# One decoder layer on one core: layer norms worked in pairs of tiles, a start in half chunks behind constant products, and later state evacuations

## The chip, the cores and the metric

The kernel runs on one core of a Trainium2 chip. The metric is the device time of one execution in microseconds (us), as the median of several runs. The engines are TensorE (PE, with its weight loads as PEld), VectorE (DVE), ScalarE (ACT), GpSimd (POOL) and SyncE (SP), whose queue (SPq) issues DMA transfers.

## The reference, cut to what matters

One macaron layer with three post-norms, for 320 tokens (256 of a prompt and 8 x 8 samples) of width 2048:

```python
x <- LN1(alpha*x + 0.5*SwiGLU_1(x))
x <- LN2(alpha*x + W_out [ retention_heads(x) ; nsa_heads(x) ])
x <- LN3(alpha*x + 0.5*SwiGLU_2(x))
```

LN takes mean and variance over the 2048 features of each token, and applies a gain and an offset per feature. The outputs are y, the retention states of prompt and samples (`rsp`, `rss`), and the new cache rows. The layers between (compressed, selected and window attention, and the retention heads) are the same in both kernels.

## The kernel before

**Data.** Activations are held transposed: 16 tiles of 128 features x 320 tokens. Every float32 operand is cut into a high half (rounded by ScalarE, L219) and a low half (source minus high, VectorE, L220), and a product is three matmuls: high weight by high x, high weight by low x, low weight by high x (`mm3`, L213 to L215). Weights come in chunks of 128x1024 (512 KB) through SyncE's queue into a ring of four (`w_load`, L269), are split two chunks ahead (`w_split`), and feed 24 matmuls each: two feature tiles of x by four output tiles, one output tile after the other. Tiles `xh` and `xl` are the halves of x.

**Stages.** `all` runs in order: `start`, FFN1 (up sweeps, then four down sweeps), LN1, the compressed cache, the combined input projection and its heads, `w_out`, LN2, FFN2, LN3 and the store of y. A main generator writes the weight matmuls. Background tasks (`spawn`) are written between them when a planner's clock, a sum of assumed matmul times, has passed their due time (`tick`). `until` and `drain` run the tasks until a condition holds or none is left. So the written order is fixed when the program is built, and each engine follows its own list.

**A layer norm.** `ln_residual` makes d = coef*x for each of the 16 tiles. `ln_evac` (L456) adds the sweep's result from PSUM. `ln_accumulate` squares the tile (ScalarE, L436) and GpSimd adds tile and square into two accumulators (L444, L445); the last four tiles go to TensorE themselves. The sums over features are matmuls against a constant tile `ones` (1/256), in full float32 (L208): a pair (d and its square) for the accumulators and one for each of the last four tiles, ten in all, four of them written in the last sweep and six after it:

```python
            if j != 1:
                self.ln_sum()
...
        while self.ln_n < 5:
            self.ln_sum()
```

`ln_stats` then makes the centre `dl` (ScalarE, L513), its square (L515), the variance (VectorE, L517), the root (ScalarE, L519), subtracts `dl` from the first tiles (L522: the first on VectorE, the others on GpSimd) and takes the reciprocal `rs` (VectorE, L524). A tile is centred (`ln_center`, L528), scaled by gain and `rs` in one VectorE operation (`ln_scale`, L531), and for LN2 split with the offset added (`ln_split`, ScalarE L539 and VectorE L540).

LN1 is done by a background task with no tile ahead, and its tiles are scaled by `x_scale`. LN2 runs by `ln_tiles`: four steps ahead of FFN2, then three in front of each chunk (`pre`), centring on GpSimd. LN3 has 13 tiles ahead (12 on GpSimd), then per tile a scale, an offset (ScalarE L1843, every sixth on VectorE, L1841) and a 160 KB transfer (L1844).

**States.** `states` makes the samples' new retention states, four heads of eight batches: per two batches two products (TensorE) into one PSUM bank, and a VectorE evacuation of 128x512 that adds the decayed state (L1711). The last head waits for `ln2_begun`, and `drain` puts it wholly ahead of FFN2.

**Start.** x comes in eight transfers of two tiles, the first four weight chunks between them. The first two x tiles are split, then the whole first chunk (ScalarE 128x1024, then VectorE), then two more tiles and the second chunk. `ones` is written at the end of the first sweep (`constants`).

## Time and profile before

| | |
|---|---|
| median of 3 runs | 2848.97 us (2848.24 to 2850.14) |
| the profiled execution | 2848.41 us |
| its span on the core | 2846.8 us |
| mean granted clock of TensorE | 0.992 |
| TensorE busy | 2784.3 us, 98% |
| VectorE busy | 1555.9 us, 55% |
| ScalarE busy | 1205.5 us, 42% |
| GpSimd busy | 351.4 us, 12% |

The span runs from the first to the last event of the core in the profiled execution, and the device time holds a little more than it. Positions below are microseconds from the span's start. Start: 0 to 12. LN1's sums: 940 to 955. LN2: 1862 to 1895. LN3 and the store: 2817 to 2847.

### The profile page before, as it was taken

How to read it: one execution, taken by the hardware profiler on the slowest of the kernel's cores; microseconds unless marked ns; L12 is line 12 of the kernel's file. 1: busy time of each engine (PE TensorE's matmuls, PEld its weight loads, DVE VectorE, ACT ScalarE, POOL GpSimd, SP SyncE). 2: the span in 40 equal slices, each digit the busy share in tenths (PEclk: the TensorE clock that was granted, in tenths of full speed). 3: DMA queues.
4: the chain of work that ended last, by engine and by line, in shares of the span. 5: the costliest groups of instructions: out<-in, count | busy, mean ns of one | idle time of the engine just before them, and what ended most of it. 6: DMA issues, size and time to landing. Idle time of an engine off the chain costs nothing. (4 is left out here: it accounts for less than half of the span.)

```text
span 2846.8 us, 49623 instructions
## 1 busy us (share of the span) xinstructions
PE 2784.3 (98%) x19841; PEld 2708.5 (95%) x19841; DVE 1555.9 (55%) x1937; ACT 1205.5 (42%) x1668; POOL 351.4 (12%) x420
## 2 busy tenths in 40 slices
PE   9999999999999999999999999999999999999996
PEld 9999999999999989998888888989999999999996
DVE  4333333347867769783565555673333333367665
ACT  4333333345445546554344454343333333354553
POOL 0000000000112223223132111440000000001111
PEclk9999999999999999999999999999999999999998
DMA  6555444446556445537577764544444444444442
GB/s 226 179 193 180 152 149 148 150 161 194 201 172 227 142 139 156 147 126 267 189 245 235 239 219 142 205 144 148 151 151 151 149 149 151 152 145 147 151 151 89
DMA packets 202600, 484.74 MB, mean 170 GB/s; under 512 B 24257, under 2 KB 100930, under 8 KB 200450
## 3 DMA queue, kind: packets, MB, share of 16 engines
q1 hardware_dynamic: 192546, 451.30, 49.3%
q0 software_dynamic: 9824, 30.29, 3.1%
q8 instruction: 155, 2.54, 0.4%
q14 instruction: 75, 0.61, 0.1%
HBM read 467.47 MB, written 22.28 MB: 172 GB/s over the span
## 5 line engine op out<-in xcount | busy, mean ns | idle before, releaser
L220 DVE TENSOR_TENSOR wl<-raw,wh 128x1024 fp32r<-128x1024 f32 x650 | 815.5, 1255 | 1073.2 <-ACT wh L219 1052.4
L219 ACT ACTIVATE wh<-raw 128x1024 fp32r<-128x1024 f32 x650 | 688.0, 1059 | 1165.2 <-PE m L214 1125.1
L213 PE MATMUL m<-x,wh 128*128 128x320 f32 x3664 | 1148.6, 313 | 10.1 <-ACT wh L219 6.3
L214 PE MATMUL m<-x,wh 128*128 128x320 f32 x3664 | 1132.9, 309 | 4.3 <-DVE x L540 4.3
L215 PE MATMUL m<-x,wl 128*128 128x320 f32 x3664 | 1132.5, 309 | 0.4 <-DVE wl L220 0.4
L213 PEld LDWEIGHTS m<-x,wh 128*128 128x128 f32 x3664 | 690.6, 188 | 33.3 <-issue 22.0
L214 PEld LDWEIGHTS m<-x,wh 128*128 128x128 f32 x3664 | 690.8, 189 | 6.3 <-DVE x L540 5.6
L215 PEld LDWEIGHTS m<-x,wl 128*128 128x128 f32 x3664 | 690.3, 188 | 0.8 <-DVE wl L220 0.8
L213 PE MATMUL m<-r,wh 128*128 128x320 f32 (+1 forms) x1592 | 495.5, 311 | 2.3 <-ACT wh L219 1.0
L214 PE MATMUL m<-r,wh 128*128 128x320 f32 (+1 forms) x1592 | 487.8, 306 | 4.4 <-DVE r L220 4.4
L215 PE MATMUL m<-r,wl 128*128 128x320 f32 (+1 forms) x1592 | 490.8, 308 | 0.0
L213 PEld LDWEIGHTS m<-r,wh 128*128 128x128 f32 x1592 | 298.7, 188 | 8.4 <-issue 3.7
L214 PEld LDWEIGHTS m<-r,wh 128*128 128x128 f32 x1592 | 299.3, 188 | 6.7 <-DVE r L220 5.8
L215 PEld LDWEIGHTS m<-r,wl 128*128 128x128 f32 x1592 | 298.3, 187 | 0.0
L476 POOL TENSOR_TENSOR t<-x,x 128x320 f32<-128x320 f32 x3 | 2.7, 913 | 1415.0 <-DVE x L456 719.1
L220 DVE TENSOR_TENSOR r<-G,r 128x640 fp32r<-128x640 f32 (+1 forms) x184 | 158.0, 863 | 0.0
L213 PE MATMUL x<-r,G 128*128 128x256 f32 x480 | 137.8, 287 | 0.0
L214 PE MATMUL x<-r,G 128*128 128x256 f32 x480 | 135.7, 283 | 0.0
L215 PE MATMUL x<-r,G 128*128 128x256 f32 x480 | 135.3, 282 | 0.0
L219 ACT ACTIVATE r<-G 128x640 fp32r<-128x640 f32 (+1 forms) x184 | 130.1, 712 | 0.0
L220 DVE TENSOR_TENSOR r<-x,r 128x512 fp32r<-128x512 f32 (+1 forms) x76 | 79.2, 1049 | 36.5 <-ACT r L219 35.7
L213 PEld LDWEIGHTS x<-r,G 128*128 128x128 f32 x480 | 91.7, 191 | 1.1 <-issue 1.0
(384 smaller groups left out, 2246.7 us busy)
## 6 DMA issues: line engine op xcount, KB each, us to landing
raw<-wup SPq DMA_DIRECT2D x352, 512.0 KB
raw<-wdn SPq DMA_DIRECT2D x176, 512.0 KB
raw<-win_ret SPq DMA_DIRECT2D x48, 512.0 KB
raw<-win_nsa SPq DMA_DIRECT2D x40, 512.0 KB
raw<-wout SPq DMA_DIRECT2D x32, 512.0 KB
r<-pks SPq DMA_DIRECT2D x96, 128.0 KB
x<-pkc SPq DMA_DIRECT2D x152, 64.0 KB
K<-cw1k SPq DMA_DIRECT2D x16, 512.0 KB
```

What stands on the lines that cost most here:

```text
L213: mm(out, wh, xh, start=start, stop=False)
L214: mm(out, wh, xl, start=False, stop=False)
L215: mm(out, wl, xh, start=False, stop=stop)
L219: self.nc.scalar.activation(hi, src, AF.Copy)
L220: self.nc.vector.tensor_tensor(lo, src, hi.bitcast(F32), op=ALU.subtract)
L476: nc.gpsimd.tensor_tensor(s, self.d[0], self.d[1], op=ALU.add)
```

## The change

1. *Start.* The first chunk comes in two transfers of 512 columns, and is split in halves in alternation with the first two x tiles. `ones` is written first, and TensorE does eleven float32 products of it with itself (`WARM`) into a PSUM bank that is overwritten later.
2. *Sums.* VectorE adds tiles 12 to 14 into one, and squares 12 to 14 into one (four additions). TensorE does two sums in the last sweep and four after it: both for the mean first, then both for the squares.
3. *Pairs.* d is allocated by pairs of tiles. `ln_stats` centres three or four pairs ahead (the first on VectorE, the others on GpSimd), each by one 128x640 operation whose second operand is repeated (`twice`). Pairs are then centred and scaled by VectorE, and gain and offset are applied by ScalarE (`ln_affine`). For LN2 `ln_pairs` does the first pair tile by tile as before. For the later ones ScalarE makes the 640-wide high half and VectorE the low one by a subtraction. Three steps stand ahead of FFN2, then one in front of each chunk. For LN3 each pair leaves in one 320 KB transfer. LN1's tiles are still scaled one by one.
4. *States.* The last head's products are written as before, but its four evacuations stand 35 planner microseconds later and 3 apart; FFN2 begins when the products are written.

```diff
@@ start
         for q in range(8):
-            self.nc.sync.dma_start(out=self.xraw[q], in_=self.I["xT"][:, 2 * q:2 * q + 2, :])
-            if q < 4:
+            if q:
+                self.nc.sync.dma_start(out=self.xraw[q], in_=self.I["xT"][:, 2 * q:2 * q + 2, :])
+            else:
+                r, w = self.raw[:, 0], self.wq[0]
+                self.nc.sync.dma_start(out=self.xraw[0], in_=self.I["xT"][:, 0:2, :])
+                for k in range(2):
+                    self.nc.sync.dma_start(out=r[:, 512 * k:512 * k + 512], in_=w[:, 512 * k:512 * k + 512])
+                self.raws[0], self.n_dma = r, 1
+            if 0 < q < 4:
                 self.w_load()
-        for q in range(2):
-            self.x_split(q)
-            self.w_split()
+        self.ones = self.t([128, 128], "ones")
+        self.nc.vector.memset(self.ones, 1.0 / 256.0)
+        ps = self.p("m3")
+        for _ in range(WARM):
+            self.nc.tensor.matmul(ps[:, 0:128], self.ones, self.ones, start=True, stop=True)
+        hi, lo = (self.t([128, 1024], t, F32R) for t in ("wh0", "wl0"))
+        r = self.raws.pop(0)
+        for k in range(2):
+            c = slice(512 * k, 512 * k + 512)
+            self.split(self.xh[k], self.xl[k], self.xraw[0][:, k])
+            self.split(hi[:, c], lo[:, c], r[:, c])
...
+        self.x_split(1)
+        self.w_split()
@@ ln_residual
+        for p in range(KT // 2):
...
+            d = self.x_room(self.kl, [128, 2, NT])
+            self.pairs[p] = d
@@ ln_accumulate
-        if m >= 12:
+        if m == 12:
+            self.ln_last = [(self.d[m], sq)]
+        elif m == 13:
+            t = self.t([128, NT], "t", bufs=NTMP)
+            nc.vector.tensor_tensor(t, self.ln_last[0][0], self.d[m], op=ALU.add)
+            nc.vector.tensor_tensor(sq, self.ln_last[0][1], sq, op=ALU.add)
+            self.ln_last = [(t, sq)]
+        elif m == 14:
+            t, q = self.ln_last[0]
+            nc.vector.tensor_tensor(t, t, self.d[m], op=ALU.add)
+            self.ln_q = q, sq
+        elif m == 15:
+            q, r = self.ln_q
+            nc.vector.tensor_tensor(q, q, r, op=ALU.add)
             self.ln_last.append((self.d[m], sq))
@@ ln_evac
-            if j != 1:
-                self.ln_sum()
+                for ps, src in zip(self.ln_sums, (self.acc_d, self.acc_q)):
+                    self.mm(ps[:, :NT], self.ones, src, True, False, 0.54)
@@ ln_stats
-    def ln_stats(self, eps, ahead=4):
+    def ln_stats(self, eps, ahead=3):
-        while self.ln_n < 5:
-            self.ln_sum()
+        for k, last in ((0, False), (0, True), (1, False), (1, True)):
+            self.mm((p1, p2)[k][:, :NT], self.ones, self.ln_last[last][k], False, last, 0.54)
-        for m in range(ahead):
-            d = self.d[m]
-            (nc.gpsimd if m else nc.vector).tensor_tensor(d, d, self.dl, op=ALU.subtract)
+        for p in range(ahead):
+            self.ln_center_pair(p, nc.gpsimd if p else nc.vector)
+    def twice(self, a):
+        return a.rearrange("p (o t) -> p o t", o=1).to_broadcast([128, 2, NT])
+    def ln_center_pair(self, p, engine):
+        d = self.pairs[p]
+        engine.tensor_tensor(d, d, self.twice(self.dl), op=ALU.subtract)
+    def ln_scale_pair(self, p):
+        if p >= self.ln_ahead:
+            self.ln_center_pair(p, self.nc.vector)
+        d = self.pairs[p]
+        self.nc.vector.tensor_tensor(d, d, self.twice(self.rs), op=ALU.mult)
+    def ln_affine(self, m, col, out, engine=None):
+        scale, bias = (self.vecs[:, c + m:c + m + 1] for c in (col, col + KT))
+        if engine is None:
+            self.nc.scalar.activation(out, self.d[m], AF.Identity, bias=bias, scale=scale)
+        else:
+            engine.tensor_scalar(out, self.d[m], scale, bias, op0=ALU.mult, op1=ALU.add)
@@ ln_tiles becomes ln_pairs
+    def ln_pairs(self, col):
...
+        for p in range(n + 1):
+            if p < n:
+                h = highs[p] = self.x_room(self.kh, [128, 2, NT], F32R)
...
+                    if p:
+                        self.ln_affine(m, col, y[p][:, k])
+                    else:
+                        self.ln_scale(m, col, y[p][:, k])
+                        nc.scalar.activation(h[:, k], y[p][:, k], AF.Identity, bias=self.ln_offset(m, col))
+                if p:
+                    nc.scalar.activation(h, y[p], AF.Copy)
...
+            q = p - 1
+            if q >= 0:
...
+                if q:
+                    nc.vector.tensor_tensor(l, y.pop(q), h.bitcast(F32), op=ALU.subtract)
...
+            if p + 1 < n:
+                self.ln_scale_pair(p + 1)
+            yield
@@ states
+                banks.append((b, pb))
+                if h < 3:
+                    self.state_out(h, sin, banks)
+                    yield 1.5
+            if h == 3:
+                self.states_begun = True
+                yield 35.0
+                while banks:
+                    self.state_out(h, sin, banks)
+                    yield 3.0
@@ all
-        tiles = self.ln_tiles(32)
-        for _ in range(4):
-            next(tiles)
+        pairs = self.ln_pairs(32)
+        for _ in range(3):
+            next(pairs)
         self.ln2_begun = True
-        self.drain()
+        self.until(lambda: self.states_begun)
         def pre(c):
-            for _ in range(3):
-                next(tiles, None)
+            next(pairs, None)
...
-        self.ln_stats(1, 13)
...
+        self.ln_stats(1, 4)
+        for p in range(KT // 2):
+            self.ln_scale_pair(p)
+            for m in (2 * p, 2 * p + 1):
+                self.ln_affine(m, 64, self.d[m], nc.vector if m == KT - 1 else None)
+            nc.sync.dma_start(out=self.O["y"][:, 2 * p:2 * p + 2], in_=self.pairs[p])
```

TensorE at the end of LN2's last sweep. Names of matmuls are `result<-moving,constant`; m is the last output tile, `t` and `x` are the squares and tiles of d, G are the states' operands. Before:

```order
L215 MATMUL m_1649_19639<-x_952_13377,wl_1651_19647 128x320
L208 MATMUL x_1657_19718<-x_1478_18290,ones_367 128x320
L208 MATMUL x_1658_19719<-t_19729,ones_367 128x320
L208 MATMUL x_1657_19718<-x_1481_18331,ones_367 128x320
L208 MATMUL x_1658_19719<-t_19738,ones_367 128x320
L208 MATMUL x_1657_19718<-x_1483_18335,ones_367 128x320
L208 MATMUL x_1658_19719<-t_19749,ones_367 128x320
L208 MATMUL x_1670_19781<-G_1282_16672,G_1583_19121 128x256 x2
L208 MATMUL x_1671_19785<-G_1282_16672,G_1583_19121 128x256 x2
```

After:

```order
L217 MATMUL m_1635_19639<-x_946_13385,wl_1637_19647 128x320
L210 MATMUL x_1643_19718<-t_19731,ones_114 128x320
L210 MATMUL x_1643_19718<-x_1469_18334,ones_114 128x320
L210 MATMUL x_1644_19719<-t_19729,ones_114 128x320
L210 MATMUL x_1644_19719<-t_19751,ones_114 128x320
L210 MATMUL x_1658_19792<-G_1276_16680,G_1569_19121 128x256 x2
L210 MATMUL x_1659_19795<-G_1276_16680,G_1569_19121 128x256 x2
L210 MATMUL x_1660_19798<-G_1276_16680,G_1570_19122 128x256 x2
```

Six sums between the last weight matmul and the states' products have become four, the two for the mean first (one on the combined tile `t_19731`, one on tile 15).

VectorE behind LN2's variance. `ln` holds the centre and the reciprocal, `vecs` gain and offset, r are the states. Before:

```order
L517 SCALAR_TENSOR_TENSOR t_19760<-x_1658_19719,t_19758 128x320
L522 TENSOR_TENSOR x_1418_17879<-x_1418_17879,ln_17813 128x320
L524 RECIPROCAL ln_17813<-t_19762 128x320
L531 SCALAR_TENSOR_TENSOR t_19769<-x_1418_17879,vecs_372,ln_17813 128x320
L531 SCALAR_TENSOR_TENSOR t_19771<-x_1420_17883,vecs_372,ln_17813 128x320
L540 SCALAR_TENSOR_TENSOR x_1667_19773<-t_19769,vecs_372,x_932_13282 128x320
L531 SCALAR_TENSOR_TENSOR t_19776<-x_1430_17977,vecs_372,ln_17813 128x320
L540 SCALAR_TENSOR_TENSOR x_1669_19778<-t_19771,vecs_372,x_934_13286 128x320
L1711 SCALAR_TENSOR_TENSOR r_1582_19119<-r_1582_19119,x_1670_19781 128x512
L1711 SCALAR_TENSOR_TENSOR r_1582_19119<-r_1582_19119,x_1671_19785 128x512
L1711 SCALAR_TENSOR_TENSOR r_1582_19119<-r_1582_19119,x_1672_19789 128x512
L1711 SCALAR_TENSOR_TENSOR r_1582_19119<-r_1582_19119,x_1673_19793 128x512
```

After:

```order
L553 SCALAR_TENSOR_TENSOR t_19761<-x_1644_19719,t_19759 128x320
L567 TENSOR_TENSOR x_1413_17889<-x_1413_17889,ln_17821 128x640
L559 RECIPROCAL ln_17821<-t_19763 128x320
L588 SCALAR_TENSOR_TENSOR G_1652_19769<-x_1413_17889,vecs_387,ln_17821 128x320 x2
L574 TENSOR_TENSOR x_1424_17986<-x_1424_17986,ln_17821 128x640
L629 SCALAR_TENSOR_TENSOR x_1655_19780<-G_1652_19769,vecs_387,x_1653_19770 128x320 x2
L574 TENSOR_TENSOR x_1430_18051<-x_1430_18051,ln_17821 128x640
L626 TENSOR_TENSOR x_1657_19788<-G_1652_19769,x_1654_19776 128x640
L567 TENSOR_TENSOR x_1438_18118<-x_1438_18118,ln_17821 128x640
L574 TENSOR_TENSOR x_1438_18118<-x_1438_18118,ln_17821 128x640
L222 TENSOR_TENSOR wl_1663_19805<-raw_63,wh_1662_19804 128x1024
L626 TENSOR_TENSOR x_1665_19813<-G_1652_19769,x_1656_19784 128x640
```

The centre has become 640 wide, the evacuations L1711 no longer stand between the first four low halves (now L629) and the split of the next weight chunk (L220, now L222), and the second pair's scale (L574) stands ahead of the first pair's low halves.

VectorE behind LN3's variance. Before:

```order
L517 SCALAR_TENSOR_TENSOR t_28181<-x_2495_28140,t_28179 128x320
L522 TENSOR_TENSOR x_2200_25233<-x_2200_25233,ln_25210 128x320
L524 RECIPROCAL ln_25210<-t_28183 128x320
L531 SCALAR_TENSOR_TENSOR x_2200_25233<-x_2200_25233,vecs_372,ln_25210 128x320
L531 SCALAR_TENSOR_TENSOR x_2203_25244<-x_2203_25244,vecs_372,ln_25210 128x320
L531 SCALAR_TENSOR_TENSOR x_2206_25255<-x_2206_25255,vecs_372,ln_25210 128x320
L531 SCALAR_TENSOR_TENSOR x_2209_25266<-x_2209_25266,vecs_372,ln_25210 128x320
L531 SCALAR_TENSOR_TENSOR x_2215_25285<-x_2215_25285,vecs_372,ln_25210 128x320
L531 SCALAR_TENSOR_TENSOR x_2217_25295<-x_2217_25295,vecs_372,ln_25210 128x320
```

After:

```order
L553 SCALAR_TENSOR_TENSOR t_28145<-x_2459_28103,t_28143 128x320
L567 TENSOR_TENSOR x_2173_25206<-x_2173_25206,ln_25181 128x640
L559 RECIPROCAL ln_25181<-t_28147 128x320
L574 TENSOR_TENSOR x_2173_25206<-x_2173_25206,ln_25181 128x640
L574 TENSOR_TENSOR x_2178_25227<-x_2178_25227,ln_25181 128x640
L574 TENSOR_TENSOR x_2186_25256<-x_2186_25256,ln_25181 128x640
L574 TENSOR_TENSOR x_2189_25275<-x_2189_25275,ln_25181 128x640
L567 TENSOR_TENSOR x_2194_25301<-x_2194_25301,ln_25181 128x640
L574 TENSOR_TENSOR x_2194_25301<-x_2194_25301,ln_25181 128x640
```

The sixteen single scales by gain and reciprocal (L531) have become pair scales (L574), preceded by a centre (L567) from the fifth pair on.

## Rows read from the trace of the kernel before

**Rows 1.** The first section of the page (busy time, share of the span, instructions), with the engines of the whole run:

```profile
PE 2784.3 (98%) x19841; PEld 2708.5 (95%) x19841; DVE 1555.9 (55%) x1937; ACT 1205.5 (42%) x1668; POOL 351.4 (12%) x420
```

**Rows 2.** The chain of waits of TensorE over the whole run (line, what was waited for: total us, times, longest us):

```profile
PE m L208 <- DVE x L821: 8.0, 2, 5.8
...
PE m L214 <- DVE x L540: 4.3, 5, 1.1
```

**Rows 3.** The timeline of the start, all engines (start in us, duration in us, engine, line, operation, number of instructions in the row, and in brackets the idle time before and what ended it):

```profile
3.87 0.83 ACT L219 ACTIVATE x<-G 128x320 fp32r<-128x320 f32 x2 [1.71 <-DMA G<-xT]
...
5.24 1.06 ACT L219 ACTIVATE wh<-raw 128x1024 fp32r<-128x1024 f32 x1 [0.54 <-DMA raw<-wup]
...
6.33 1.23 DVE L220 TENSOR_TENSOR wl<-raw,wh 128x1024 fp32r<-128x1024 f32 x1 [1.06 <-ACT wh L219]
...
6.35 0.64 PE L213 MATMUL m<-x,wh 128*128 128x320 f32 x1 [6.35 <-ACT wh L219]
...
7.61 0.64 PE L215 MATMUL m<-x,wl 128*128 128x320 f32 x1 [0.36 <-DVE wl L220]
...
8.84 0.47 PE L213 MATMUL m<-x,wh 128*128 128x320 f32 x1
...
11.51 0.31 PE L214 MATMUL m<-x,wh 128*128 128x320 f32 x1
...
11.65 0.31 PE L215 MATMUL m<-x,wl 128*128 128x320 f32 x1
```

**Rows 4.** The timeline after LN1's first sums, on TensorE, ScalarE and the queue of SyncE (columns as in rows 3):

```profile
946.12 0.70 PE L208 MATMUL x<-x,ones 128*128 128x320 f32 x2
...
950.90 0.38 PE L214 MATMUL m<-r,wh 128*128 128x256 f32 x1 [1.69 <-DVE r L220]
...
1019.32 1.06 ACT L219 ACTIVATE r<-x 128x1024 fp32r<-128x1024 f32 x1 [8.52 <-DMA x<-pkc]
...
950.89 32.28 SPq L609 DMA_DIRECT2D x<-pkc  x48
```

**Rows 5.** The timeline at LN2, TensorE first, then ScalarE, VectorE and GpSimd (columns as in rows 3; L208 with `ones` are the sums, L208 with G are the states' products, the x of L213 to L215 are FFN2's first matmuls):

```profile
1871.61 0.70 PE L208 MATMUL x<-x,ones 128*128 128x320 f32 x2
...
1874.84 3.62 PE L208 MATMUL x<-G,G 128*128 128x256 f32 x16
...
1880.46 0.42 PE L213 MATMUL m<-x,wh 128*128 128x320 f32 x1 [2.00 <-ACT x L539]
...
1884.14 0.64 PE L214 MATMUL m<-x,wh 128*128 128x320 f32 x1 [0.98 <-DVE x L540]
...
1891.36 0.42 PE L214 MATMUL m<-x,wh 128*128 128x320 f32 x1 [0.84 <-DVE x L540]
...
1874.56 0.44 ACT L513 ACTIVATE ln<-x 128x320 f32<-128x320 f32 x1 [1.70 <-PE x L208]
...
1871.81 0.49 DVE L456 TENSOR_TENSOR x<-x,m 128x320 f32<-128x320 f32 x1 [1.47 <-PE m L215]
...
1875.36 0.49 DVE L517 SCALAR_TENSOR_TENSOR t<-x,t 128x320 f32<-128x320 f32 x1 [3.06 <-ACT t L515]
...
1876.55 2.15 DVE L524 RECIPROCAL ln<-t 128x320 f32<-128x320 f32 x1 [0.26 <-ACT t L519]
...
1878.73 2.14 DVE L531 SCALAR_TENSOR_TENSOR t<-x,vecs,ln 128x320 f32<-128x320 f32 x2
...
1884.01 2.47 DVE L1711 SCALAR_TENSOR_TENSOR r<-r,x 128x512 f32<-128x512 f32 x4
...
1890.77 0.54 DVE L540 SCALAR_TENSOR_TENSOR x<-t,vecs,x 128x320 fp32r<-128x320 f32 x1
...
1860.65 1.86 POOL L444 TENSOR_TENSOR ln<-ln,x 128x320 f32<-128x320 f32 x1
...
1877.79 12.71 POOL L528 TENSOR_TENSOR x<-x,ln 128x320 f32<-128x320 f32 x12
```

**Rows 6.** Stretches of LN2 (busy time and instructions of each engine, then the granted clock of TensorE as a share of full speed, DMA share, GB/s):

```profile
1878.40:1881.90 3.50, 0.47 (x2) 0.19 (x1) 3.46 (x5) 1.55 (x3) 3.50 (x5) 1.00 0.00 0
...
1881.90:1888.70 6.80, 5.72 (x20) 5.33 (x21) 6.80 (x10) 1.08 (x2) 6.80 (x7) 0.51 0.22 93
```

**Rows 7.** Single operations elsewhere that are as wide as the new ones: ScalarE and VectorE splits of 640 columns (columns as in rows 3), and by shape, with its mean in ns, a VectorE operation whose second operand is repeated along the row:

```profile
2809.92 0.73 ACT L219 ACTIVATE r<-G 128x640 fp32r<-128x640 f32 x1
...
2807.67 0.82 DVE L220 TENSOR_TENSOR r<-G,r 128x640 fp32r<-128x640 f32 x1
...
L1522 DVE TENSOR_TENSOR G<-G,sc 128x512 f32<-128x512 f32 x8 | 5.5, 683 | 0.0
```

**Rows 8.** The timeline after FFN2, VectorE and ScalarE (columns as in rows 3), then the GpSimd centres and the output's transfers by source line (ns min/median/max, first and last start):

```profile
2825.36 0.49 DVE L517 SCALAR_TENSOR_TENSOR t<-x,t 128x320 f32<-128x320 f32 x1 [3.06 <-ACT t L515]
...
2826.55 2.15 DVE L524 RECIPROCAL ln<-t 128x320 f32<-128x320 f32 x1 [0.26 <-ACT t L519]
...
2828.74 6.39 DVE L531 SCALAR_TENSOR_TENSOR x<-x,vecs,ln 128x320 f32<-128x320 f32 x6
...
2843.16 0.56 ACT L1843 ACTIVATE x<-x,vecs 128x320 f32<-128x320 f32 x1 [0.43 <-DVE x L531]
...
L522 POOL TENSOR_TENSOR x<-x,ln x12: 853/1102/1105, 2825.1 to 2835.8; 128x320 f32<-128x320 f32 x12
...
L1844 SPq DMA_DIRECT2D y<-x x16: 332/332/404, 2830.4 to 2843.7; - x16
```

More of the change, by code (lines that the diff above doesn't have):

```diff
@@ L25 @@
 PAST = 2048
+WARM = 11
 NTMP = 5
@@ L416, in ln_begin @@
         self.d = [None] * KT
+        self.pairs = [None] * (KT // 2)
         self.ln_last = []
-        self.ln_n, self.ln_banks = 0, banks
+        self.ln_banks = banks
         self.ln_first, self.ln_shifted = True, False
@@ L424, in ln_residual @@
         nc = self.nc
-        for m in range(KT):
-            t1 = self.t([128, NT], "t", bufs=NTMP)
-            nc.scalar.activation(t1, self.xl[m].bitcast(F32), AF.Copy, scale=coef)
-            d = self.x_room(self.kl, [128, NT])
-            nc.vector.scalar_tensor_tensor(d, self.xh[m].bitcast(F32), coef, t1, op0=ALU.mult, op1=ALU.add)
-            self.d[m] = d
-            yield 0.8
+        for p in range(KT // 2):
+            t1 = [self.t([128, NT], "t", bufs=NTMP) for _ in range(2)]
+            for k in range(2):
+                nc.scalar.activation(t1[k], self.xl[2 * p + k].bitcast(F32), AF.Copy, scale=coef)
+            d = self.x_room(self.kl, [128, 2, NT])
+            self.pairs[p] = d
+            for k in range(2):
+                nc.vector.scalar_tensor_tensor(d[:, k], self.xh[2 * p + k].bitcast(F32), coef, t1[k], op0=ALU.mult, op1=ALU.add)
+                self.d[2 * p + k] = d[:, k]
+                yield 0.8
     def ln_accumulate(self, m):
@@ L540, in ln_split @@
         self.nc.vector.scalar_tensor_tensor(self.xl[m], y, b, self.xh[m].bitcast(F32), op0=ALU.add, op1=ALU.subtract)
-    def ln_tiles(self, col):
-        y = {}
-        for step in range(KT + 2):
-            if step < KT:
-                self.ln_center(step, self.nc.gpsimd)
-            m = step - 1
-            if 0 <= m < KT:
-                y[m] = self.t([128, NT], "t", bufs=NTMP)
-                self.ln_scale(m, col, y[m])
-            m = step - 2
-            if m >= 0:
-                self.xl[m] = self.x_room(self.kl, [128, NT], F32R)
-                self.ln_split(m, col, y.pop(m))
-            yield 1.3
+    def ln_pairs(self, col):
+        nc = self.nc
+        ys = self.t([128, 6, NT], "G7")
+        y, highs = {}, {}
+        n = KT // 2
+        for p in range(n + 1):
+            if p < n:
+                h = highs[p] = self.x_room(self.kh, [128, 2, NT], F32R)
+                y[p] = ys[:, 2 * (p % 3):2 * (p % 3) + 2]
+                for k in range(2):
+                    m = 2 * p + k
+                    if p:
[5 more added lines that the diff above has]
+                    nc.scalar.activation(h, y[p], AF.Copy)
+                self.xh[2 * p:2 * p + 2] = h[:, 0], h[:, 1]
+            q = p - 1
+            if q >= 0:
+                l = self.x_room(self.kl, [128, 2, NT], F32R)
+                h = highs.pop(q)
+                if q:
+                    nc.vector.tensor_tensor(l, y.pop(q), h.bitcast(F32), op=ALU.subtract)
+                else:
+                    for k in range(2):
+                        nc.vector.scalar_tensor_tensor(l[:, k], y[0][:, k], self.ln_offset(k, col), h[:, k].bitcast(F32), op0=ALU.add, op1=ALU.subtract)
+                self.xl[2 * q:2 * q + 2] = l[:, 0], l[:, 1]
+            if p + 1 < n:
+                self.ln_scale_pair(p + 1)
+            yield
     def constants(self):
         nc = self.nc
-        self.ones = self.t([128, 128], "ones")
-        nc.vector.memset(self.ones, 1.0 / 256.0)
         self.eps = self.t([128, 2], "eps")
@@ L1832, in all @@
         self.drain()
-        self.ln_stats(1, 13)
-        for step in range(KT + 1):
-            if step < KT:
-                self.ln_center(step, nc.vector)
-                self.ln_scale(step, 64, self.d[step])
-            if step:
-                m = step - 1
-                if m % 6 == 4:
-                    nc.vector.tensor_scalar(self.d[m], self.d[m], self.ln_offset(m, 64), None, op0=ALU.add)
-                else:
-                    nc.scalar.activation(self.d[m], self.d[m], AF.Identity, bias=self.ln_offset(m, 64))
-                nc.sync.dma_start(out=self.O["y"][:, m], in_=self.d[m])
+        self.ln_stats(1, 4)
[4 more added lines that the diff above has]
+            nc.sync.dma_start(out=self.O["y"][:, 2 * p:2 * p + 2], in_=self.pairs[p])
     def w_out(self):
```

22 lines of the change are left out of this document (10 added, 12 removed).

## The prediction

> **What bounds the kernel now.** I read the busy table first: TensorE is busy 98% of the span [rows 1]. A change that leaves the weight matmuls as they are can only win where TensorE waits, where it runs at half clock, or at the two ends of the span, before its first and after its last matmul. So I next read its chain of waits for the lines that the change touches [rows 2], and then the timeline at the four places: the start, LN1, LN2 and the output after LN3 [rows 3, 4, 5, 8]. The sum is made against the profiled run: 2848.41 us, 1.6 over its span of 2846.8, and 0.56 under the median of the runs, which I take as noise.
>
> **The start.** Before, the first matmul starts at 6.35, released by the 1.06 us ScalarE split of a whole chunk, and the third waits until 7.61 for VectorE's half of it [rows 3]. The 7th starts at 8.84 and the 17th at 11.51: 0.267 each, half clock. From 11.51 to 11.65 it is 0.14, the pitch of full clock. After: x tile 0 lands as before, at 3.87; a whole chunk came 1.37 later (5.24), half of one comes about 0.7 later, 4.6. ScalarE splits 512 columns in about 0.6 (1.06 for 1024), VectorE in about 0.67 (1.23): first real matmul 5.3, first `wl` half 6.0, then tile 1 and the second half in the same alternation, the last `wl` half at 7.05. The 6th matmul waits for it; the 7th starts at 7.3.
>
> The 11 products are fp32, two instructions each. One 320-column pair took 0.54 at full clock (L208, six pairs from 1871.61 to 1874.84) [rows 4, 5], so 0.27 an instruction, and for 128 columns at half clock 0.267 x 2 x 128/320 = 0.21: 22 of them 4.7 us, from about 1.1 to 5.8, just as data arrive. If they bring the clock up as the first real matmuls did, the 17th matmul starts at 7.3 + 10 x 0.145 = 8.75 against 11.51: 2.75 gained. If they do nothing for it and the 17th is again the first at full pitch, it starts at 7.3 + 10 x 0.267 = 9.95, and 1.5 is gained. If a product instruction costs as much as the 0.267 of a half-clock matmul of 320 columns, 22 take 5.9 and the first real matmul is at 7.0; the 17th is then at 9.3 at full clock (2.2 gained) or at 11.3 at half (0.2). I take 2.5, since nothing in the rows tells a product from a real matmul, and keep 0.2 to 2.8.
>
> **LN1's sums.** Four pairs of sums fewer are 4 x 0.54 = 2.2 us of TensorE. But right behind them it waits 1.69 for a VectorE split at 950.90 [rows 4], whose chain hardly moves, and further on ScalarE sits 8.52 us until a page load lands at 1019.32, with TensorE waiting 5.8 of it [rows 2, 4]. The page loads are issued back to back on SyncE's queue, 48 in 32.28 us; a TensorE that arrives 2 us earlier waits 2 us longer there. I take 0; bounds 2.2 gained (if the loads come earlier too) and 1.7 lost (a longer wait with half clock behind it).
>
> **LN2.** Before: last sweep's end 1871.61, six sums to 1874.84, `dl` 1874.56, variance 1875.36, reciprocal 1876.55 to 1878.70. Then VectorE's L531 take 1.07 apiece (2.14 for two) because GpSimd centres twelve tiles from 1877.79 on for 12.71 us; alone such an operation takes 0.54 long and 0.46 apart [rows 5]. TensorE's first FFN2 matmul waits 2.00, the fifth starts at 1884.14 and the 29th at 1891.36, behind the four state evacuations of 2.47. Granted clock: 1.00 in 1878.4 to 1881.9 while TensorE does 0.47 us of work in 3.5, then 0.51 until 1888.7 [rows 6], the lower level.
>
> After: two sums less ahead of the sweep's end (1870.53). The combined tiles cost VectorE four more additions of about 0.49 (as L456) and are ready near 1871.4, so TensorE waits 0.9, does four sums to 1873.6, and the variance comes at 1873.87, 1.5 earlier. The pair's centre (0.75, below) stands ahead of the reciprocal: 1875.6 to 1877.75. GpSimd has two pairs, from 1873.3 to 1877, and is out of the way. Then y0, y1 at 0.46 each to 1878.8, ScalarE's `xh` of tile 0 at 1878.95, the scale of pair 1 (0.75), `xl` 0 and 1 to 1880.5. The fifth matmul starts at 1880.55 instead of 1884.14: 3.6 gained. The state evacuations are 35 us later, on a VectorE that then has room; before they stood between the fifth matmul and the 29th. With no other wait the 29th comes 24 matmuls on: 1884.05 at full clock (7.3 gained), 1886.95 at half clock (4.4). TensorE is idle some 2.8 us between the states' products (to 1877.1) and 1880.55, less than the 2.00 + 1.1 + 0.98 of before [rows 2, 5], so I take the middle, 5.8; bounds 4.0 and 7.3. Per chunk VectorE then has centre 0.8, scale 0.75, subtraction 0.75 and split 1.15: 3.45 against 24 x 0.145 = 3.5 of TensorE. That just holds. Head 3's state goes out on SyncE's queue behind some 15 more weight loads; its issue waits for the last evacuation as before, and the loads behind it run chunks ahead, so I cost it at nothing (a chunk late would cost 3.5).
>
> **The price of a pair operation.** Nothing of before runs 128x640 with a repeated operand. A plain 640-column VectorE operation took 0.82 [rows 7], about 0.75 apart; one with a repeated operand took 0.683 for 512 [rows 7], 0.85 scaled. I take 0.75 to 0.84. Two single ones cost 0.92 to 1.0.
>
> **The output after LN3.** The variance moves from 2825.36 to 2823.87, the reciprocal's end to 2827.75 as at LN2. Before, six L531 take 6.39 beside GpSimd's twelve centres (1102 ns beside VectorE, 853 alone), then seven singles follow; the last ScalarE step starts at 2843.16 and the span ends 3.0 after that step's end [rows 8]. After, GpSimd has three pairs, about 1.65 each (2 x 0.85), from 2823.3 to about 2828.4. From there VectorE does four pair scales (3.0) and four times centre and scale (0.84 + 0.75): 9.4, to 2837.8; last ScalarE step to 2838.4. The last transfer is 320 KB instead of 160; at the start 512 KB took 1.37 [rows 3], so 0.4 more: end 2838.4 + 3.0 + 0.4 = 2841.8. Gain 5.0; bounds 3.7 and 6.4 (twelve operations at 0.06 either way, GpSimd's 0.4, the transfer's 0.3).
>
> Here the two engines share. A VectorE operation of 0.46 and a GpSimd one of 0.853 done by turns would take 1.31 a round; side by side a round took 1.07 to 1.10 [rows 5, 8], so they overlap a little, and GpSimd slows VectorE by 0.6 per centre. The Trainium skill, SBUF — State Buffer, section "Who interferes with whom", calls the shared port pair an exclusive lock held for the whole instruction by whoever issues first, and puts two-input VectorE operations among those that contend. That speaks against wider GpSimd operations: each then blocks for 1.65. The trace does not show whole blocking. By the page VectorE's first two pair operations would each wait for a GpSimd pair's end, some 0.5 more, and the sum would be 12.8 instead of 13.3.
>
> **Other parts.** Moving `ones` to the front costs one small VectorE operation that hides in the wait for x (3.87 [rows 3]). The output's eight issues instead of sixteen (332 ns each [rows 8]) lie beside VectorE.
>
> Sum: 2.5 + 0 + 5.8 + 5.0 = 13.3; 2848.4 - 13.3 = 2835.1, say **2835.0**.
>
> **The rivals.**
> 1. *Half clock at LN2.* It falls there as before (4.4 instead of 5.8): 11.9, 2836.5; with the start's 1.5 as well 2837.5. For it: rows 6, where a mostly idle 3.5 us went ahead of the fall. Against: the idle time after is half as long. The Trainium skill, TensorE: Matmul & The Clock Gate, section "HAM oscillation — how this bites in real kernels", lets a wait between two bursts of matmuls send TensorE back to its lower clock, at which the next burst begins. By that rule the time is this rival's 2836.5; rows 6 agree for the longer gap, and no row of before shows the shorter one.
> 2. *More.* LN1's 2.2 count and LN2 stays at full clock (7.3): 17.0, 2831.4. For it: the shorter gap. Against: SyncE's queue is full throughout.
> 3. *No change.* Pair operations with a repeated operand are no faster than two singles: 1.2. Twelve at LN3 lose 5 of 5; at LN2 two on the path and eighteen in the chunks, at 0.46 each against no slack, cost 9 of 5.8: 2848 or so. Against: the 683 ns row.
> 4. *Slower.* Since a pair is one buffer, the odd tile's evacuation would wait for GpSimd's additions of the even one, up to 1.86 each [rows 5]; about 18 such tiles in three norms at 1.8 are 32 us, 2867. It decides above 13.3/18 = 0.74 a tile. Against: by the kernel's written waits that evacuation waits for VectorE and TensorE alone.
>
> **How the numbers follow.** The forecast has 65%, rivals 1 to 4 have 14, 10, 6 and 5. The forecast's own range is 2832 to 2838.5; rivals 1 and 2 lie in or beside it, and the bounds of all terms together (gains of 6.2 to 18.7) give 2830 to 2842, which leaves out 3, 4 and little else. 0.2%, 5.7 us, is about what a measurement of this kernel can tell from no change. Faster is 0.89, same 0.06, slower 0.05.
>
> **What would show it.** Right: a 7th matmul near 7.3 with 0.145 behind it; FFN2's fifth matmul near 1878 (1880.55 less the start's 2.5) and the 29th within 5 us of it; no state evacuation in between; 128x640 operations at 0.75 to 0.9; from LN3's variance to the span's end 17.9 instead of 21.4. Wrong: 640-wide operations above 1.1, new waits of TensorE on VectorE once per chunk in FFN2's first sweep, waits for L498, or SyncE's page loads ending earlier at LN1.

## The result

The changed kernel takes 2836.35 us (median of 6 runs, 2831.34 to 2837.85) against 2849.55 before: ratio 0.9949, interval 0.9936 to 0.9962, so 13.2 us faster where 13.3 was forecast (2835.0). The ratio is estimated from all the runs, it is not the quotient of the two medians (0.9954). Timed a second time against fifteen runs of before, the ratio was 0.9932 (0.9919 to 0.9946). The profiled run took 2837.03, span 2835.4, 11.4 under the span before.

The busy table of the changed kernel: TensorE is 6 us less busy, the rest of the gain is idle time.

```profile
PE 2778.3 (98%) x19839; PEld 2704.3 (95%) x19839; DVE 1553.6 (55%) x1933; ACT 1212.1 (43%) x1677; POOL 335.4 (12%) x398
```

Its chain of waits holds a wait of 1.7 for a ScalarE split (L221, at LN1) and one for the sums' additions (L474), neither of which before had, and shorter ones at LN2 than [rows 2, 5]:

```profile
PE m L215 <- ACT r L221: 2.3, 3, 1.7
...
PE x L210 <- DVE t L474: 1.7, 2, 0.8
...
PE m L215 <- ACT x L617: 1.5, 1, 1.5
...
PE m L216 <- DVE x L629: 0.7, 1, 0.7
```

**Start** (timeline, columns as in [rows 3]). The eleven products are the first row, ScalarE's split of the first half chunk the second; the 1st, 6th, 7th and 17th real matmul follow, with the split of the second chunk (7.97) among them, and last a weight load of TensorE that waits for that chunk's low half:

```profile
1.20 4.68 PE L347 MATMUL m<-ones 128*128 128x128 f32 x22 [1.20 <-DVE ones L344]
...
4.56 0.63 ACT L221 ACTIVATE wh<-raw 128x512 fp32r<-128x512 f32 x1 [0.17 <-DMA raw<-wup]
...
5.64 0.39 PE L215 MATMUL m<-x,wh 128*128 128x320 f32 x1
...
6.97 0.41 PE L217 MATMUL m<-x,wl 128*128 128x320 f32 x1 [0.19 <-DVE wl L222]
7.23 0.31 PE L215 MATMUL m<-x,wh 128*128 128x320 f32 x1
...
7.97 1.06 ACT L221 ACTIVATE wh<-raw 128x1024 fp32r<-128x1024 f32 x1 [0.41 <-DMA raw<-wup]
...
8.69 0.31 PE L216 MATMUL m<-x,wh 128*128 128x320 f32 x1
...
10.34 0.19 PEld L217 LDWEIGHTS m<-x,wl 128*128 128x128 f32 x1 [0.28 <-DVE wl L222]
```

The products take 4.68 and the 7th matmul comes at 7.23, at 0.145 apart from there on: the 17th at 8.69 instead of 11.51, 2.82 earlier. Of these 0.3 go again at 10.34, in a wait for the second chunk that before had not.

**LN1** (timeline, then two stretches with the granted clock). The wait of [rows 4] is still there (947.94), but one of 1.71 for ScalarE's split now stands just ahead of it, and behind both the matmuls run at the lower clock:

```profile
945.87 0.38 PE L215 MATMUL m<-r,wh 128*128 128x256 f32 x1 [1.71 <-ACT r L221]
...
947.94 0.58 PE L216 MATMUL m<-r,wh 128*128 128x256 f32 x1 [1.68 <-DVE r L222]
...
943.00:947.40 4.40, 1.54 (x11) 1.14 (x9) 3.29 (x6) 3.95 (x8) 0.00 (x0) 1.00 0.52 160
947.40:951.00 3.60, 3.06 (x15) 3.06 (x16) 3.60 (x6) 1.49 (x2) 1.69 (x3) 0.53 0.49 163
```

**LN2** (timeline; then the stretch that was at 0.51 in [rows 6]). The first row is the wait for the additions, 1881.50 is the fifth matmul:

```profile
1872.47 0.81 PE L210 MATMUL x<-t,ones 128*128 128x320 f32 x2 [0.83 <-DVE t L474]
...
1879.88 0.41 PE L215 MATMUL m<-x,wh 128*128 128x320 f32 x1 [1.54 <-ACT x L617]
...
1880.95 0.41 PE L216 MATMUL m<-x,wh 128*128 128x320 f32 x1 [0.65 <-DVE x L629]
...
1881.50 0.33 PE L216 MATMUL m<-x,wh 128*128 128x320 f32 x1
...
1874.98 0.49 DVE L553 SCALAR_TENSOR_TENSOR t<-x,t 128x320 f32<-128x320 f32 x1 [1.77 <-ACT t L551]
1875.39 1.19 DVE L567 TENSOR_TENSOR x<-x,ln 128x640 f32<-128x640 f32 x1
1876.51 2.14 DVE L559 RECIPROCAL ln<-t 128x320 f32<-128x320 f32 x1
...
1881.90:1888.70 6.80, 6.80 (x49) 6.80 (x47) 5.96 (x8) 6.10 (x9) 0.00 (x0) 1.00 0.18 45
```

The granted clock stays at 1.00, and TensorE has no wait after the second matmul.

**LN3 and the output** (timeline, then the pair operations by source line, ns min/median/max):

```profile
2817.57 0.49 DVE L553 SCALAR_TENSOR_TENSOR t<-x,t 128x320 f32<-128x320 f32 x1 [1.77 <-ACT t L551]
...
2821.26 3.67 DVE L574 TENSOR_TENSOR x<-x,ln 128x640 f32<-128x640 f32 x4
...
2831.35 0.65 ACT L580 ACTIVATE x<-x,vecs 128x320 f32<-128x320 f32 x1 [0.40 <-DVE x L574]
...
L574 DVE TENSOR_TENSOR x<-x,ln x8: 810/824/1466, 2821.3 to 2830.5; 128x640 f32<-128x640 f32 x8
...
L567 POOL TENSOR_TENSOR x<-x,ln x3: 1528/1533/2114, 2817.0 to 2820.5; 128x640 f32<-128x640 f32 x3
```

From the variance to the span's end it is 17.8 (2817.57 to 2835.4), before 21.4.

### The profile page after: what moved, and what is told of

It is laid out like the page before. It is cut to its first block, busy times and chain, and to the rows that moved or that the text cites. A ratio compares the mean times of both kernels' runs of the same rounds, so it can differ in the third digit from the quotient of the medians.

```text
span 2835.4 us, 49605 instructions
## 1 busy us (share of the span) xinstructions
PE 2778.3 (98%) x19839; PEld 2704.3 (95%) x19839; DVE 1553.6 (55%) x1933; ACT 1212.1 (43%) x1677; POOL 335.4 (12%) x398
## 5 line engine op out<-in xcount | busy, mean ns | idle before, releaser
L222 DVE TENSOR_TENSOR wl<-raw,wh 128x1024 fp32r<-128x1024 f32 (+1 forms) x651 | 815.6, 1253 | 1067.3 <-ACT wh L221 1054.5
L221 ACT ACTIVATE wh<-raw 128x1024 fp32r<-128x1024 f32 (+1 forms) x651 | 688.1, 1058 | 1164.8 <-PE m L216 1125.8
L215 PE MATMUL m<-x,wh 128*128 128x320 f32 x3664 | 1144.4, 312 | 3.3 <-ACT x L617 1.5
L215 PEld LDWEIGHTS m<-x,wh 128*128 128x128 f32 x3664 | 688.1, 188 | 26.7 <-issue 22.2
L215 PE MATMUL m<-r,wh 128*128 128x320 f32 (+1 forms) x1592 | 495.2, 311 | 4.0 <-ACT r L221 2.3
L215 PEld LDWEIGHTS m<-r,wh 128*128 128x128 f32 x1592 | 298.9, 188 | 9.9 <-issue 3.7
L222 DVE TENSOR_TENSOR r<-G,r 128x640 fp32r<-128x640 f32 (+1 forms) x184 | 155.5, 849 | 0.0
L215 PE MATMUL x<-r,G 128*128 128x256 f32 x480 | 137.6, 287 | 0.0
L221 ACT ACTIVATE r<-G 128x640 fp32r<-128x640 f32 (+1 forms) x184 | 130.1, 712 | 0.0
L222 DVE TENSOR_TENSOR r<-x,r 128x512 fp32r<-128x512 f32 (+1 forms) x76 | 79.5, 1053 | 35.9 <-ACT r L221 34.6
L215 PEld LDWEIGHTS x<-r,G 128*128 128x128 f32 x480 | 91.8, 191 | 1.0 <-issue 1.0
```

Of the source, the lines that this page charges most:

```text
L215: mm(out, wh, xh, start=start, stop=False)
L221: self.nc.scalar.activation(hi, src, AF.Copy)
L222: self.nc.vector.tensor_tensor(lo, src, hi.bitcast(F32), op=ALU.subtract)
```

## The experiments

All traces were compared at the same ScalarE splits of 1024 columns (weight chunks and page tiles, the same rows in every kernel behind the first chunk), which gives the lead over the first trace of before at any place. For example the split at 1019.32 [rows 4] stands at 1017.30 in the changed kernel: a lead of 2.0. The table gives how much lead was won in each stretch (negative: lost). The bounds are the splits near 898, 959, 1862 and 2809 of before, and the span's end.

| kernel | start to FFN1 | LN1 | middle (caches, heads, W_out) | LN2 | LN3 and output | span |
|---|---|---|---|---|---|---|
| changed | 2.5 | -0.6 | -2.8 | 7.4 | 4.9 | 11.4 |
| after_again | 2.3 | -0.9 | 1.3 | 7.4 | 4.9 | 15.0 |
| before_again | 0.1 | 0.0 | 1.5 | 0.0 | 0.0 | 1.7 |
| start_only | 2.6 | 0.0 | 2.4 | 0.1 | 0.0 | 5.1 |
| old_start | 0.3 | -0.7 | 1.6 | 7.4 | 4.9 | 13.5 |
| warm0 | 0.5 | -0.9 | 3.9 | 7.4 | 4.9 | 15.8 |
| old_sums | 2.5 | 0.0 | -0.2 | 4.3 | 3.2 | 9.8 |
| drained | 2.3 | -0.7 | -1.0 | 5.9 | 4.9 | 11.4 |
| drained_again | 1.2 | -0.9 | -3.3 | 6.2 | 4.9 | 8.2 |
| states_only | 0.2 | 0.0 | 2.3 | 1.1 | 0.0 | 3.6 |
| old_tiles | 1.7 | -1.9 | 4.4 | 2.5 | 4.9 | 11.6 |
| old_ln3 | 1.3 | -0.8 | 5.1 | 6.1 | 1.7 | 13.5 |
| better | 2.0 | 0.0 | 3.1 | 5.9 | 4.4 | 15.3 |

Outside the middle the same code gives nearly the same number each time at LN3 (4.9 in seven traces), one of two numbers at LN2 (by the clock, below), -0.6 to -0.9 and once -1.9 at LN1, and 1.2 to 2.6 at the start. So a part is judged by its own stretch and against the scatter there, and not by whole times, which scatter by several us.

### The middle: is 2.8 lost there by the change?

Two kernels were run once more, unaltered.

> The changed kernel once more, unaltered, for a second trace. In the first one the changed kernel was 2.0 us ahead of the kernel before behind the page loads of LN1 and 1.0 us behind it at the end of W_out: 3 us went in TensorE's waits for gathered transfers between them. Theory A (the transfers set the pace there, whatever comes ahead): the second trace shows the same 3 us again within 0.5, time 2836 to 2837. Theory B (chance of one execution): the stretch from LN1 to LN2 differs from the first trace by more than 1.5 us, and the time goes with it, towards 2833 to 2834.

Measured: 2832.3 (2830.19 to 2834.38), middle +1.3 where the first trace had -2.8: theory B.

> The kernel before, unaltered, for a second trace. If the waits of TensorE for gathered transfers are fixed by the program, the second trace repeats them (0.65 for cw1k, 0.3 for pks, 2.9 for pvs, together 3.9 to 4.9) and the span from the page loads to the end of W_out within 0.5 us; if they are chance, they differ by more than 1 us.

Measured: 2846.73, middle +1.5 against its own first trace, with nothing changed.

The middle goes by chance: two traces of the same kernel differ by 1.5 to 4.1 there, and over all the kernels, whose code is the same in the middle, the lowest (-3.3) and the highest (5.1) are over 8 us apart. Kernels with the change and without it are not told apart by it, so no loss there is shown to belong to the change. It is probably also the largest part of why one run of this kernel can differ by several us from the next.

### The start

`start_only` has the whole new start and `old_start` the whole old one; the lines below show one loop of each.

```diff
# start_only: the kernel before with
+        for _ in range(WARM):
+            self.nc.tensor.matmul(ps[:, 0:128], self.ones, self.ones, start=True, stop=True)
...
# old_start: the changed kernel with
+        for q in range(2):
+            self.x_split(q)
+            self.w_split()
...
# warm0: the changed kernel with
-WARM = 11
+WARM = 0
```

> The kernel before with the new start alone (first chunk in halves, constant products); all else as before. Theory A (the middle waits for transfers and eats what the start gains): no change, within 0.5 us of before, although the 17th matmul starts 2.5 to 2.8 earlier. Theory B (the gain stays to the end): 2.3 to 2.8 us faster, 2847 beside 2849.5.

Measured: 2846.47 against 2849.47, ratio 0.999 (0.9981 to 0.9999); 2.6 won at the start and not lost again in its trace. Theory B; the interval of the times alone only just excludes no change.

> The changed kernel with the old start (whole first chunk, no constant products); sums, pairs and states as changed. Theory A (the middle eats the start's gain): as the changed kernel, 2836 to 2837. Theory B (it stays): 2.3 to 2.8 slower than the changed kernel, about 2839.

Measured: 2838.75 (5 runs), lead at the start 0.3, the other stretches outside the middle as in the changed kernel. B again by the stretch. The time is 2.40 above the changed kernel's first median and 6.45 above its second, so times do not settle it.

> The changed kernel without the eleven constant products. Theory A (they bring the clock up): matmuls run 0.267 apart from the first on, the 17th starts at 9.9 to 10.2 instead of 8.7, so 1.2 to 1.5 slower. Theory B (the halved chunk is the whole gain of the start): the 17th within 0.3 of 8.7.

Measured: 2834.61 (4 runs), between the two medians of the changed kernel, so that the time does not show the loss; the stretch does. The start's lead is 0.5. The timeline of TensorE in warm0, the 1st, 7th, 20th, 21st and 22nd matmul:

```profile
5.23 0.64 PE L215 MATMUL m<-x,wh 128*128 128x320 f32 x1 [5.23 <-ACT wh L221]
...
7.71 0.47 PE L215 MATMUL m<-x,wh 128*128 128x320 f32 x1
...
11.18 0.47 PE L216 MATMUL m<-x,wh 128*128 128x320 f32 x1
11.45 0.45 PE L217 MATMUL m<-x,wl 128*128 128x320 f32 x1
11.71 0.33 PE L215 MATMUL m<-x,wh 128*128 128x320 f32 x1
```

The 7th is 1.1 earlier than before, but the matmuls stay 0.267 apart until 11.7, where before it was 11.5 [rows 3]. The 17th lies at 10.4, a little later than expected. So in this one trace halves without products bring 0.5, against 2.3 and 2.5 in the two traces of the changed kernel, and the products the other 1.8 to 2.0. Theory A, and more than it asked for: without them the early start was mostly spent at half clock.

The start's gain is 1.2 to 2.6 over the nine traces with halves and products. In drained_again, the lowest, ScalarE waits for the second half's landing, which it did not in the changed kernel, then for the second chunk, and behind the first chunk TensorE waits 0.58 for the second:

```profile
6.29 0.63 ACT L221 ACTIVATE wh<-raw 128x512 fp32r<-128x512 f32 x1 [0.66 <-DMA raw<-wup]
...
9.26 1.06 ACT L221 ACTIVATE wh<-raw 128x1024 fp32r<-128x1024 f32 x1 [0.56 <-DMA raw<-wup]
...
11.63 0.41 PE L217 MATMUL m<-x,wl 128*128 128x320 f32 x1 [0.58 <-DVE wl L222]
```

The second chunk sets the gain: ScalarE's split of it starts at 7.88 in start_only (2.60 won), at 7.97 in the changed kernel (2.47), at 8.73 in old_tiles (1.74) and at 9.26 in drained_again (1.21). In all nine the two add up to 10.43 to 10.48, so what this chunk lands later is lost of the gain. In eight of the nine TensorE waits for it, and 0.2 to 0.9 of what the 17th matmul had won is gone by the 49th; in old_sums it just does not. The second half does not order the traces: its split starts latest in old_tiles (6.45).

### The sums

```diff
-        if m == 12:
-            self.ln_last = [(self.d[m], sq)]
-        elif m == 13:
...
+        if m >= 12:
+            self.ln_last.append((self.d[m], sq))
...
-        for k, last in ((0, False), (0, True), (1, False), (1, True)):
+        while self.ln_n < 5:
+            self.ln_sum()
```

> The changed kernel with the ten sums per norm of before (no additions on VectorE for tiles 12 to 14). Theory A (the four sums fewer leave TensorE idle at LN1 and the granted clock falls to 0.5 behind it): no half clock behind LN1's sums, and the stretch of LN1 as in the kernel before, 0.7 to 0.9 better than changed; LN2 and LN3 lose 1.3 each (2.15 of sums, less the 0.83 that TensorE waits for the additions). Together 1.8 slower. Theory B (the fall at LN1 comes from elsewhere in the change): it stays, and 2.6 is lost.

Measured: 2839.38 (10 runs), ratio 0.9968. LN1 loses nothing and its clock stays up, as the same two stretches show:

```profile
943.00:947.40 4.40, 3.66 (x23) 2.94 (x21) 2.07 (x3) 3.07 (x6) 0.43 (x1) 1.00 0.61 202
947.40:951.00 3.60, 2.60 (x22) 2.60 (x23) 3.60 (x7) 1.96 (x3) 1.98 (x4) 1.00 0.51 159
```

In the first stretch TensorE is busy for 3.66 of 4.4 us, in the changed kernel for 1.54: with 2.2 less work it comes to the matmul at 945.87 before ScalarE's split for it is done and waits 1.71 there, ahead of the wait that before had too. All eight traces with the new sums at LN1 show this second wait and the fall, and lose 0.6 to 1.9; all five with ten sums show neither and lose 0.0. Theory A; that the idle time is the link is read from the waits and the two busy shares, and was not tried apart from the sums. LN3 loses 1.7 without the new sums (1.3 expected). LN2 loses 3.1, but there the clock falls in old_sums (0.50 from 1879.7 to 1881.7) and not in the changed kernel; against kernels in which it falls too (better and old_ln3, below) it is 1.5 to 1.8.

### LN2: evacuations, clock, pairs

```diff
# drained: the changed kernel with
-                if h < 3:
+                if True:
...
-                yield 35.0
...
-        self.until(lambda: self.states_begun)
+        self.drain()
...
# old_tiles: the changed kernel with
-        pairs = self.ln_pairs(32)
+        tiles = self.ln_tiles(32)
...
# states_only: the kernel before with
...
-        self.drain()
+        self.until(lambda: self.states_begun)
```

> The changed kernel with the last head's four state evacuations written ahead of FFN2 again (no 35 us delay); all else as changed. The second pair's low half ended 1.1 us ahead of its use there. Theory A (the evacuations on VectorE are what TensorE waited for after LN2's first matmuls): 2.5 us of VectorE work come back, 1.1 hidden, so TensorE waits 1.4 or more at the third chunk, and if the clock falls there up to 4 are lost. Theory B (the shorter chain and the idle GpSimd give the whole gain): within 0.3 us from LN2's last sweep to FFN2's end.

Measured: 2837.32 (7 runs). LN2 5.9, so 1.5 lost, but not by the wait of theory A, nor within the 0.3 of B: TensorE has no new wait, and runs at half clock in the stretch in which FFN2 begins:

```profile
1879.40:1882.80 3.40, 3.40 (x13) 3.40 (x14) 2.99 (x5) 3.34 (x7) 0.00 (x0) 0.52 0.00 0
```

> The same kernel as drained, for a second trace: evacuations ahead of FFN2. In the first trace TensorE had no new wait, but its granted clock was 0.5 for 3.4 us from FFN2's first matmuls on, and 1.5 was lost. The clock also fell there in one kernel whose LN2 is exactly that of the changed one, and stayed up in four others. Theory A (chance): this trace may keep the clock up; then a wait of up to 0.6 shows at the third chunk and the stretch gains 6.8 to 7.4. Theory B (the evacuations bring the fall about): it falls again, 5.9.

Measured: 2840.23 in one run. The clock stays up this time (the stretch from FFN2's second matmul on), and the evacuations show as a wait at the third chunk, 0.93; LN2 6.2, so they cost 1.2.

```profile
1882.80:1886.00 3.20, 3.04 (x20) 3.02 (x21) 2.82 (x5) 3.14 (x6) 0.00 (x0) 1.00 0.00 0
...
1891.22 0.41 PE L216 MATMUL m<-x,wh 128*128 128x320 f32 x1 [0.93 <-DVE x L626]
```

Theory A for the clock, with a wait over its bound of 0.6 and a gain under its 6.8. The clock's fall is not fixed by the program here: TensorE's rows up to FFN2's second matmul are those of the changed kernel in both traces (waits of 0.83, 1.54 and 0.65). Over all the kernels with pairs and new sums at LN2, the clock stays up in five (changed, after_again, old_start, warm0, drained_again) and falls in three (drained, old_ln3, better). Where it falls, LN2 brings 5.9 to 6.1 instead of 7.4. In drained, where it falls, the evacuations show no cost of their own.

> The kernel before with the last head's evacuations 35 us later and nothing else changed. Before, TensorE waited 0.23 and 0.84 for VectorE's low halves behind the four evacuations of 2.47. Theory A (the evacuations hold up the low halves): those two waits go and the stretch from LN2's last sweep to FFN2's end is 1.1 to 2.5 shorter. Theory B (the tile scales beside GpSimd hold them up anyway): 0 to 0.5.

Measured: 2844.8 in one run. LN2 1.1, the lower end of A, but of its two waits only the one of 0.23 is gone; of 0.84 a 0.79 is left, so that the scales beside GpSimd (theory B) hold up the low halves as well:

```profile
1881.62 0.64 PE L214 MATMUL m<-x,wh 128*128 128x320 f32 x1 [0.98 <-DVE x L540]
...
1887.74 0.41 PE L214 MATMUL m<-x,wh 128*128 128x320 f32 x1 [0.79 <-DVE x L540]
```

> The changed kernel with LN2's factors worked tile by tile as before (four steps ahead, then three before each chunk, centres on GpSimd); sums, later evacuations, start and LN3 as changed. From LN2's last sweep to FFN2's end the changed kernel gained 7.4. Theory A (the pairs, which take GpSimd's centres from beside VectorE, give most of it): VectorE's scales are 1.07 apart again and FFN2's fifth matmul comes only about 1.5 earlier than before; with the evacuations out of the way 3 to 4 of the 7.4 stay, so 3.5 to 4.5 are lost. Theory B (sums and evacuations give most): at most 1.5 is lost.

Measured: 2839.65 (10 runs), LN2 2.5: without the pairs 4.9 of the 7.4 are lost. Theory A, even beyond it. A part of the 4.9 is the clock, which is at half in old_tiles from 1876.0 to 1882.8 (0.50), as it was before [rows 6]. Against the kernels with pairs in which the clock falls too (better and old_ln3, 5.9 and 6.1) 3.3 to 3.6 are left. The first two scales and FFN2's fifth matmul, in the trace of old_tiles:

```profile
1873.30 1.67 DVE L610 SCALAR_TENSOR_TENSOR t<-x,vecs,ln 128x320 f32<-128x320 f32 x2
...
1878.25 0.63 PE L216 MATMUL m<-x,wh 128*128 128x320 f32 x1 [0.98 <-DVE x L619]
```

With a lead of 4.2 ahead of LN2, the fifth matmul at 1878.25 is 1.7 earlier than the 1884.14 of [rows 5]; in the changed kernel 1881.50 with a lead of -1.0 is 3.6 earlier. The losses without sums, without late evacuations and without pairs (3.1, 1.2, 4.9) add up to more than 7.4, since the clock is in more than one of them.

### The output

```diff
-        for p in range(KT // 2):
-            self.ln_scale_pair(p)
...
+        for step in range(KT + 1):
+            if step < KT:
...
+                self.ln_scale(step, 64, self.d[step])
```

> The changed kernel with the output of before: twelve single centres on GpSimd, a scale by gain and reciprocal per tile on VectorE, sixteen transfers. From the first sum of FFN2's last sweep to the span's end the kernel before took 30.0 us and the changed one 25.0. Theory A (the gain is the pairs and the three centres of GpSimd): 28.6, that is 30.0 less the 1.4 of the sums; 3.6 slower. Theory B (half of it is the shorter last transfers or the sums): 27 or less.

Measured: 2838.36 (10 runs). From the first sum to the span's end it takes 28.3 (2805.02 to 2833.3), 3.2 more than changed. Theory A. The 3.2 and the 1.7 of the sums make up the 4.9. Whether the wider operations or the fewer centres on GpSimd bring the 3.2 was not tried apart.

### Both findings put together

`ten` is true in the first norm alone.

```diff
+        if self.ten and m >= 12:
+            self.ln_last.append((self.d[m], sq))
...
-        self.ln_stats(1, 4)
+        self.ln_stats(1, 5)
```

> The changed kernel with two differences: LN1 keeps the ten sums of before, and LN3 centres five pairs ahead instead of four (four on GpSimd). LN1: no half clock behind the sums, 0.7 to 0.9 better than changed from the last FFN1 sweep to the first page loads. LN3: one VectorE centre of 0.85 less, and GpSimd beside VectorE 1.7 longer, which slows VectorE's scales by about 0.6: 25.05 from the first sum to the span's end becomes 24.7 to 25.2. Rival: GpSimd's fourth pair ends after VectorE needs it and costs 0.5 or more. Together 0.5 to 1.2 faster than the changed kernel, less than its runs scatter.

Measured: 2835.34 (5 runs, 2832.38 to 2838.39), no different from the changed kernel in time. LN1 loses nothing, as expected. The fifth pair ahead is the rival's case: LN3 brings 4.4 instead of 4.9. GpSimd's fourth pair lies beside VectorE's scales, and five of these take 5.75, where four had taken 3.67. That is 2.08 for one scale more, 1.3 over its 0.74, against 0.85 for the centre saved:

```profile
2812.50 7.17 POOL L581 TENSOR_TENSOR x<-x,ln 128x640 f32<-128x640 f32 x4 [71.61 <-ACT ln L563]
...
2816.82 5.75 DVE L588 TENSOR_TENSOR x<-x,ln 128x640 f32<-128x640 f32 x5
```

Keeping ten sums at LN1 and four pairs ahead at LN3 is what the stretches point to, 0.8 better than changed; that combination was not run.

## Why the prediction was right

**The sum.** 2.5 + 0 + 5.8 + 5.0 was forecast. The stretches of the changed kernel gave 2.5, -0.6, 7.4 and 4.9, together 14.2, and chance in the middle took 2.8 in the profiled run and gave 1.3 in the next. The predicted time held, but two terms and one reading did not: LN2 brought 1.6 more than its term and LN1 0.6 less, and the chance in the middle took what was over. That the time came within 1.4 of the forecast is in part luck.

**Start: right in size, wrong in make-up.** The 7th matmul (7.3 forecast, 7.23) and the products (4.7, 4.68) were right, the first matmul came at 5.64 instead of 5.3, and the 17th 2.82 earlier (2.75). The forecast had no wait for the second chunk, which takes 0.3 of that again and in other traces up to 0.9; that 2.5 was taken and 2.5 came is luck. The price of halves without products was set at 1.5, on the assumption that the 17th would again be the first at full pitch; in warm0 it was the 22nd, and 0.5.

**LN1: the sign.** The step "I take 0" named the loss among its bounds ("a longer wait with half clock behind it") and then set it to nothing. That is what came: the wait for VectorE stayed (1.68, before 1.69), one of 1.71 for ScalarE came up ahead of it, behind both the clock fell, and 0.6 to 0.9 was lost, once 1.9. So the idle time came at these splits already, ahead of the page loads, where the forecast saw it. The argument that the page loads' queue would absorb any lead cannot be tested in these traces, since the stretch of those loads varies by more than 1 us with nothing changed.

**LN2: the chain exact, the clock mis-sized.** The fifth matmul was forecast 3.6 earlier and came 3.6 earlier; the variance was 1.3 earlier (1.5). The sign of a fifth matmul near 1878 failed in the first trace (1881.50, since the lead was -1.0 by then) and held in the second (1877.85). The 29th depended on the clock. The forecast took the middle, 5.8, between two states of which neither is in the middle: 7.4 without the fall, 5.9 to 6.1 with it. Rival 1, the fall, had been priced at 4.4, for which the half clock would have had to last through all 24 matmuls; in drained it lasted only from about 1879.4 to 1882.8 (0.52, then 0.98 to 1886.0). The rule of the Trainium skill, TensorE: Matmul & The Clock Gate, section "HAM oscillation — how this bites in real kernels", that a wait between two bursts of matmuls lets the clock go down, is borne out at LN1 by all eight traces with the two waits of 1.7, while none of the six with only one shows a fall; at LN2 it is borne out in three of eight with the same waits. That the pairs are the largest part was read rightly from [rows 5]: 4.9 with the clock in it. How much of this is GpSimd's centres out of the way of the scales, and how much the wider operations, was not tried apart. The state evacuations are worth 1.1 to 1.2 (0.9 of it a wait).

**The price of a pair operation.** 0.75 to 0.84 apart was forecast; they stand 0.74 apart, 0.85 where one reads what the last wrote (2826.45 to 2827.30). A repeated operand costs nothing against the plain 0.82 of [rows 7]. Rival 3 falls by that; its 1.2 was also above the 0.92 to 1.0 that the forecast itself gives two single ones.

**LN3: right sum, one reading wrong.** I read in [rows 5, 8] that the two engines overlap a little and put the lock of the Trainium skill, SBUF — State Buffer, section "Who interferes with whom", at 0.5 against the change. The runs show nearly whole blocking: VectorE's first pair scale starts at 2821.26 and takes 1466 ns, while GpSimd's last centre (1528 ns alone) is running until 2822.05; the other scales take 810. That is 0.66 more of the 0.79 that were left. The other way round one GpSimd centre took 2114 behind VectorE's. The sum came out right all the same, because it had VectorE begin only at GpSimd's end: 2828.4, which less the lead of 6.5 is 2821.9. So the rule of the Trainium skill was in the sum already, and the 0.5 for it would have been counted twice. The mis-step is the sentence that the trace does not show blocking.

**Rival 4** had no part: in no trace does an evacuation wait for GpSimd; all waits of theirs are for TensorE.

## What to carry to other kernels

Price a clock question by its two outcomes and their chances, not by the middle, and look at what TensorE loses when work is taken from it just ahead of a wait: at LN1 four sums fewer made the stretch slower. Work on GpSimd beside VectorE is not free: in better one more GpSimd centre slowed VectorE by 1.3 us and saved it 0.85. When a start is made earlier, look at what lands next: here the second chunk set the gain. Where part of a kernel scatters by several us, judge a change by its own stretch of the trace, cut at rows that both kernels have.
